# A one-core hybrid pooling / SSD encoder step: gate products in the other pool of PSUM banks, two pool tiles' sums behind gate splits, and a new order for the last piece's scalings and the last tile's weights

## The chip, the cores and the metric

The kernel runs on one core of one Trainium2 chip. The metric is the device time of one execution in microseconds (us). Engine names are those of the profile: PE multiplies matrices (TensorE; PEld is its weight load), DVE is VectorE, ACT is ScalarE, POOL is GpSimd, and SP issues most of the DMAs. PSUM is the memory that PE writes its products to. It is used here as eight banks of 128 x 512 float32, and a product occupies one bank until DVE or ACT has read it.

## The reference, cut to what matters

One layer of a streaming encoder for 384 tokens (256 of a new stream and 8 x 16 of running streams), width 2048, all in float32:

```
u = RMSNorm(x); P = u @ w_in                 # columns: pool | z | xBC | dt | gates
pool branch: for windows 2, 4, 8, 16 (four groups of 512 channels)
  d = windowed mean of p - p; a = (d @ pool_w[g]) * pool_scale
SSD branch: causal conv, Mamba-2 scan, gated RMSNorm
m = sigmoid(g_A) * (a @ w_pool_proj) + sigmoid(g_B) * (a_ssd @ w_ssd_proj)
x += RMSNorm(m @ w_out)
x += RMSNorm(relu(RMSNorm(x) @ w_up)^2 @ w_down)
outputs: y (384 x 2048), new pooling, conv and SSM states
```

## The kernel before

**Products.** Each float32 operand is cut into a high and a low part (`h`, `l`) of a type that PE takes at full rate, and each product is three matmuls: `h*h`, `h*l`, `l*h`. Activations are cut once. Weights are cut as they stream in: `wfetch` has SP fetch 128 x 1024 elements into one of three buffers of the tag `w`; `wsplit` has ACT write the high part (`wh`, line 72) and DVE the low part (`wl`, line 73), three buffers each. A product of 384 columns is 128 channels by 384 tokens (`proj`, two halves of 24 matmuls); its matmuls are lines 100, 101 and 102 of the helper `mm3`.

**Banks.** Two pools share PSUM in the first half: `mmtile` hands out two banks in turn and `sstile` six. `proj` takes its bank from whatever `bank[0]` holds, which is `mmtile` at the start.

**Pool and gate stage.** Five of the sixteen tiles of the pooling input (`early`, p0 to p4) are multiplied while the input arrives, in `sstile` banks. `pool_tile(gi, k4)` takes tile k = 4*gi + k4: DVE scales it out of its bank by the norm (lines 379 to 381), ACT copies states in and out, DVE makes the window sums (396), the difference from the mean (399 to 412) and the split (415 on ACT, 416 on DVE). `pool_map(g)` multiplies group g's four tiles by `pool_w[g]`. `gate_a(i)` multiplies gate tile i (`pj_ga`), scales it out of its bank (439) and takes the sigmoid. The program has tiles 0 to 3, tiles 4 and 5 (p5 is the first product of this stage in an `mmtile` bank), gates 0 to 3, then `pool_map(0)`.

**Order.** Instructions are recorded in the program's order and a list scheduler then sets each engine's order from dependencies and its own costs. `behind(ins)` tells it to issue something only after `ins` on that engine; `later()` does so behind the latest weight split on ACT and on DVE. On each engine the resulting order is fixed, and an instruction that waits holds up all behind it.

**The MLP's second product.** `w_down` is multiplied by a scheme with fewer products than the plain one, in eight chunks of 1024 rows and column pieces; `blocks(c, sb, w)` does one piece. Its splits have letters (a, b, c, d, e, f, g; ACT line 1363, DVE line 1364), its matmuls are lines 1377 to 1379, its banks X, Y, M and `c3`. `evict` adds a bank to `acc` (1386); the sums `t2 = w21 + t2` are line 1330. In the last chunk, `blocks(7, 0)`, a finished 128 x 512 block is also tallied: `tally` has ACT square and sum it (1310) and DVE multiply it by the post-norm's gain `gpo` (1313).

**The last two column blocks** (nb = 2 and 3) are multiplied plainly, with `w_tail`: four weight units each (`wt2_0` to `wt2_3`, `wt3_0` to `wt3_3`; matmul lines 1495 to 1497). For nb = 3 two units go to `wpool`, and units 2 and 3 are fetched there but cut into buffers of their own (`e_wt3_2`, `e_wt3_3`, lines 1519 and 1520). The products of nb = 3 are ordered by token block b = 0, 1, 2; behind each, `tally` finishes block b: `acc` (1305), the square, the gain, the norm and four outputs (1325) with their DMAs (1326).

Of the kernel before, what the change touches and what calls it, by code (L numbers as in the profile page):

```python
# [10 lines left out]
ALU = mybir.AluOpType  # L11
# [22 lines left out]
def build(ctx, tc, io):  # L34
# [93 lines left out]
    def proj(units, rhs, name, hook=None):  # L128
        o = bank[0](f"pj_{name}")[:, :T]
        for q, src in enumerate(units):  # L130
            half(o, q, take(src, f"{name}_{q}"), rhs)
            if hook:
                hook()
        return o
# [223 lines left out]
    with tc.tile_pool(name="phc", bufs=1, reuse_waits="tile") as pc, tc.tile_pool(name="phc2", bufs=2, reuse_waits="tile") as pc2:  # L358
# [9 lines left out]
        ]  # L368
        dd = [[None] * 4 for _ in range(4)]

        def pool_tile(gi, k4):
            w = WINDOWS[gi]
            k = gi * 4 + k4
            ps = early[k] if k < 5 else proj(in_units(1 + k), xg, f"p{k}")
            bf = bufs[k % 2]
            pv = bf[:, 15:271]
            sv = bf[:, 271:].rearrange("p (b t) -> p b t", b=NB)
            po = even_odd(ps)
            v.tensor_tensor(pv[:, :192], po[:, 0], rstd[:, :192], ALU.mult)
            v.tensor_tensor(pv[:, 192:], po[:, 1, :64], rstd[:, 192:TP], ALU.mult)  # L380
            v.tensor_tensor(
                sv[:, :, 15:],
                po[:, 1, 64:].rearrange("p (b t) -> p b t", b=NB),
                rstd[:, TP:].rearrange("p (b t) -> p b t", b=NB),
                ALU.mult,
            )
            s.copy(sv[:, :, :15], pst[:, k])
            stg = pc2.tile([P, 9, 15], F32, tag="stg", name=f"pstg{k}")
            s.copy(stg[:, 0, :], bf[:, 256:271])
            s.copy(stg[:, 1:, :], sv[:, :, 16:])  # L390
            gp.dma_start(io["new_pool"][k], stg)
            cur, sh = bf, 1
            while sh < w:
                nx = pc2.tile([P, 519], F32, tag="win", name=f"win{k}_{sh}")
                lo = 2 * sh - 1
                v.tensor_tensor(nx[:, lo:], cur[:, lo:], cur[:, lo - sh : 519 - sh], ALU.add)
                cur, sh = nx, sh * 2
            d = pc2.tile([P, T], F32, tag="d", name=f"d{k}")
            v.scalar_tensor_tensor(
                out=d[:, :TP], in0=cur[:, 15:271], scalar=1.0 / w, in1=pv, op0=ALU.mult, op1=ALU.subtract  # L400
            )
            v.scalar_tensor_tensor(
                out=d[:, TP:].rearrange("p (b t) -> p b t", b=NB),
                in0=cur[:, 271:].rearrange("p (b t) -> p b t", b=NB)[:, :, 15:],
                scalar=1.0 / w,
                in1=sv[:, :, 15:],
                op0=ALU.mult,
                op1=ALU.subtract,
            )
            rc = cst[:, C_RC + gi * 16 : C_RC + gi * 16 + 16]  # L410
            v.tensor_tensor(d[:, :16], cur[:, 15:31], rc, ALU.mult)
            v.tensor_tensor(d[:, :16], d[:, :16], pv[:, :16], ALU.subtract)
            h = pc.tile([P, T], F32R, tag=f"dh{k4}", name=f"dh{k}", bufs=1)
            l = pc.tile([P, T], F32R, tag=f"dl{k4}", name=f"dl{k}", bufs=1)
            s.activation(h, d, AF.Copy)
            v.tensor_tensor(l, d, h.bitcast(F32), ALU.subtract)
            dd[gi][k4] = (h, l)
# [15 lines left out]
                        out=al, in0=even_odd(o), scalar=sc, in1=ah.bitcast(F32), op0=ALU.mult, op1=ALU.subtract  # L433
                    )

        def gate_a(i):
            ps = proj([io["w_ga"][i, q] for q in range(2)], xg, f"ga{i}")
            sg = pc2.tile([P, T], F32, tag="sg", name=f"sg{i}", bufs=5)
            v.tensor_tensor(halves(sg), even_odd(ps), halves(rstd), ALU.mult)
            s.activation(sg, sg, AF.Sigmoid)  # L440
            return sg
# [76 lines left out]

        for gi in range(4):
            for k4 in range(4):  # L520
                pool_tile(gi, k4)
                if gi and k4 == (gi == 1):
                    if gi == 1:
                        sg = [gate_a(i) for i in range(4)]
                    pool_map(gi - 1, last[0])
        srcs = dt_phase(pc)
        pool_map(3)
# [713 lines left out]
    with ExitStack() as mlp:  # L1241
# [108 lines left out]
        def blocks(c, sb, w):  # L1350
# [16 lines left out]
            def run(hl, ps, *terms):  # L1367
                wh, wl = hl
                with behind(last[0]):
                    for out, j, start in terms:  # L1370
                        for p in ps:
# [6 lines left out]
                            te.matmul(o, h[:, t], vl, start=False, stop=False, skip_group_check=True)  # L1378
                            last[0] = te.matmul(o, l[:, t], vh, start=False, stop=False, skip_group_check=True)  # L1379

            def evict(b, j, src, op=ALU.add, first=False, done=False):
                dst = acc[:, b, blk(2 * sb + j)]
                if first and c == 0:
                    s.activation(dst, src, AF.Copy, scale=-1.0 if op == ALU.subtract else 1.0)
                else:
                    v.tensor_tensor(dst, dst, src, op)
                if done and c == NC - 1:
                    tally(b, 2 * sb + j, dst)

            M = mmtile(f"m{nm}")  # L1390
            a, t, b = (X, H11, True), (Y, S1, True), (M, H12, True)
# [12 lines left out]
            run(t1_, (3,), t)  # L1404
            run(b1, (3,), b, rb)
            if c == NC - 1:
                tally(2, 2 * sb, A)
            d0, d1 = split(t2, 0, "d"), split(t2, 1, "d")
            run(d0, (0, 1), (X, S2, False))
            evict(0, 1, Y, first=True)  # L1410
# [1 line left out]
            run(d1, (2, 3), (X, S2, False))  # L1412
            evict(1, 1, X, ALU.subtract, first=True)
            e0, e1 = split(w["12"], 0, "e"), split(w["12"], 1, "e")
            run(e0, (0, 1), (B, H31, c == 0))
            run(e1, (2, 3), (B, H31, False))
            run(e0, (0, 1), (X, S3, False))
# [6 lines left out]
            f1 = split(w["22"], 1, "f")  # L1424
            run(f1, (2, 3), (B, H3, False), (Y, S4, False))
            if c == NC - 1:
                tally(2, 2 * sb + 1, B)
            evict(1, 1, Y, done=True)
            for u in (0, 1):
                run(split(t2, u, "g"), (2 * u, 2 * u + 1), (X, H22, False))  # L1430
            evict(0, 0, X, first=True, done=True)

        for f in range(3):
            up(f)
# [45 lines left out]
        def lhs(i):  # L1480
# [2 lines left out]
            e = [extra[0][:, i // 2 * 256 + q : i // 2 * 256 + q + P] for q in (0, P)]  # L1483
            return [e if j is None else (h[:, j * P : j * P + P], l[:, j * P : j * P + P]) for j in js]

        for nb in (2, 3):
            o = [mmtile(f"wt{nb}_{b}") if nb == 2 else psd.tile([P, 512], F32, tag="XY"[b], name=f"wt{nb}_{b}") for b in range(2)]
            o.append(c3[nb])
# [12 lines left out]
            if nb == 2:  # L1501
                for kp in range(4):
                    hl = wload(units[kp], names[kp])
                    with behind(last[0]):
                        for i in (2 * kp, 2 * kp + 1):
                            for b in range(3):
                                mm(b, hl, i)
                for b in range(3):
                    tally(b, nb, o[b], b < 2)
                continue  # L1510
            w = []
            for kp in range(4):
                f_, name = wfetch(units[kp], names[kp])
                if kp < 2:
                    w.append(wsplit((f_, name)))
                    continue
                t = pr.tile([P, 2048], F32R, tag=f"t{kp - 1}", name=f"e_{name}")
                h, l = t[:, :1024], t[:, 1024:]
                s.activation(h, f_, AF.Copy)
                v.tensor_tensor(l, f_, h.bitcast(F32), ALU.subtract)  # L1520
                w.append((h, l))
            for b in range(3):
                with behind(last[0]):
                    for i in range(8):
# [125 lines left out]
```

## Time and profile before

| | us |
|---|---|
| median of 3 runs (2621.88 to 2622.18) | 2621.91 |
| the profiled execution's own time | 2624.44 |
| its span, first to last instruction | 2622.7 |
| PE busy | 2606.7 |
| DVE busy | 1775.3 |
| ACT busy | 1302.9 |
| mean granted PE clock (share of full) | 0.998 |

Rows of the timeline read: start, duration, engine, line, operation, output<-inputs, shapes, count, and in brackets the idle time before it with what ended it. PE's matmuls overlap, so a matmul's row is longer than its step to the next start. A row of the waits reads: who waited, for whom, us in total, times, longest.

### The profile page before, as it was taken

To read this page: it belongs to the slowest core of one execution; us is meant where nothing else is said; L and a number is where in the kernel's file an instruction comes from. 1 tells how busy PE (TensorE), PEld (TensorE's weight loads), DVE (VectorE), ACT (ScalarE), POOL (GpSimd) and SP (SyncE) were. 2 spreads that over 40 slices of the span, in tenths; PEclk is the share of its full clock that TensorE was granted. 3 is DMA by queue.
4 is the path that set the end of the run, shared out by engine and by line. 5 is a ranking of instruction groups with operands and counts; after the bars stand their busy time and mean duration, and the time that the engine had idled before them with its cause. 6 is when DMAs were issued, how large, how long until landed. Compare 5 with 4: busy or idle time off the path is not lost.

```text
span 2622.7 us, 40313 instructions
## 1 busy us (share of the span) xinstructions
PE 2606.7 (99%) x15999; PEld 2508.9 (96%) x15999; DVE 1775.3 (68%) x2383; ACT 1302.9 (50%) x1981; POOL 185.8 (7%) x264
## 2 busy tenths in 40 slices
PE   9999999999999999999999999999999999999998
PEld 8999999999999999999999998999999999999997
DVE  6676334778888887876444434766676868677677
ACT  6434225566666575744423334645454545445454
POOL 0000000001111111111000000000000000000000
PEclk9999999999999999999999999999999999999999
DMA  7444445566656666666644455543433444444343
GB/s 276 141 132 159 146 145 199 177 216 208 234 195 226 204 237 204 208 219 228 216 156 160 160 193 169 205 141 129 145 129 131 163 153 141 138 145 144 129 164 118
DMA packets 139420, 457.76 MB, mean 175 GB/s; under 512 B 17568, under 2 KB 44768, under 8 KB 125792
## 3 DMA queue, kind: packets, MB, share of 16 engines
q1 hardware_dynamic: 117120, 326.98, 38.6%
q0 software_dynamic: 22112, 128.21, 13.3%
q8 instruction: 126, 2.06, 0.3%
q14 instruction: 62, 0.51, 0.1%
HBM read 410.26 MB, written 44.86 MB: 174 GB/s over the span
## 4 chain that ended last, share of the span: by engine, by line
PE 96%; DVE 2%; ACT 1%; issue 1%; DMA 1%; POOL 0%; ACTq 0%; POOLq 0%; DVEq 0%
PE pj_up L100 6%; PE pj_up L102 6%; PE pj_up L101 6%; PE pj_x L100 4%; PE pj_x L102 4%; PE pj_x L101 4%; PE pj_z L100 3%; PE pj_z L101 3%; PE pj_sp L102 3%; PE pj_sp L101 3%; PE pj_sp L100 3%; PE pj_z L102 3%; PE c L1378 2%; PE c L1379 2%; PE X L1378 2%; PE X L1379 2%
## 5 line engine op out<-in xcount | busy, mean ns | idle before, releaser
L100 PE MATMUL pj_up<-x1h,wh_up 128*128 128x384 f32 (+1 forms) x1024 | 333.9, 326 | 0.0
L102 PE MATMUL pj_up<-x1h,wl_up 128*128 128x384 f32 (+1 forms) x1024 | 333.7, 326 | 0.0
L101 PE MATMUL pj_up<-x1l,wh_up 128*128 128x384 f32 (+1 forms) x1024 | 333.7, 326 | 0.0
L100 PE MATMUL pj_x<-xgh,wh_x 128*128 128x384 f32 x768 | 252.0, 328 | 0.0
L102 PE MATMUL pj_x<-xgh,wl_x 128*128 128x384 f32 x768 | 250.6, 326 | 0.9 <-DVE wl_x L73 0.9
L101 PE MATMUL pj_x<-xgl,wh_x 128*128 128x384 f32 x768 | 250.4, 326 | 0.0
L72 ACT ACTIVATE wh_up<-w_up 128x1024 fp32r<-128x1024 f32 x126 | 133.1, 1056 | 189.7 <-PE pj_up L101 113.8
L101 PEld LDWEIGHTS pj_up<-x1l,wh_up 128*128 128x128 f32 x1024 | 193.5, 189 | 0.4
L100 PEld LDWEIGHTS pj_up<-x1h,wh_up 128*128 128x128 f32 x1024 | 193.5, 189 | 0.4
L102 PEld LDWEIGHTS pj_up<-x1h,wl_up 128*128 128x128 f32 x1024 | 193.5, 189 | 0.0
L73 DVE TENSOR_TENSOR wl_up<-w_up,wh_up 128x1024 fp32r<-128x1024 f32 x126 | 153.6, 1220 | 58.3 <-ACT wh_up L72 57.3
L101 PE MATMUL pj_z<-xgl,wh_z 128*128 128x384 f32 x512 | 166.9, 326 | 0.0
L100 PE MATMUL pj_sp<-abh,wh_sp 128*128 128x384 f32 x512 | 166.9, 326 | 0.0
L102 PE MATMUL pj_sp<-abh,wl_sp 128*128 128x384 f32 x512 | 166.9, 326 | 0.0
L101 PE MATMUL pj_sp<-abl,wh_sp 128*128 128x384 f32 x512 | 166.9, 326 | 0.0
L102 PE MATMUL pj_z<-xgh,wl_z 128*128 128x384 f32 x512 | 166.9, 326 | 0.0
L100 PE MATMUL pj_z<-xgh,wh_z 128*128 128x384 f32 x512 | 166.9, 326 | 0.0
L73 DVE TENSOR_TENSOR wl_sp<-w_sp,wh_sp 128x1024 fp32r<-128x1024 f32 x64 | 78.2, 1222 | 116.7 <-ACT wh_sp L72 116.7
L72 ACT ACTIVATE wh_x<-w_x 128x1024 fp32r<-128x1024 f32 x96 | 101.0, 1052 | 107.0 <-PE pj_z L101 53.0
L73 DVE TENSOR_TENSOR wl_x<-w_x,wh_x 128x1024 fp32r<-128x1024 f32 x96 | 117.2, 1221 | 51.4 <-ACT wh_x L72 51.4
L72 ACT ACTIVATE wh_sp<-w_sp 128x1024 fp32r<-128x1024 f32 x64 | 67.8, 1059 | 166.4 <-PE pj_sp L101 158.3
L100 PEld LDWEIGHTS pj_x<-xgh,wh_x 128*128 128x128 f32 x768 | 145.1, 189 | 2.6 <-issue 0.4
(455 smaller groups left out, 7114.6 us busy)
## 6 DMA issues: line engine op xcount, KB each, us to landing
w_up<-w_up SPq DMA_DIRECT2D x128, 512.0 KB, 3.5
w<-w_dn POOLq DMA_DIRECT2D x60, 1024.0 KB, 5.2
w_x<-w_in SPq DMA_DIRECT2D x96, 512.0 KB, 3.9
w_z<-w_in SPq DMA_DIRECT2D x64, 512.0 KB, 3.5
w_sp<-w_ssd SPq DMA_DIRECT2D x64, 512.0 KB, 3.5
w_ga<-w_ga SPq DMA_DIRECT2D x32, 512.0 KB, 3.5
w_pp<-w_pp SPq DMA_DIRECT2D x32, 512.0 KB, 3.5
hs<-ssm POOLq DMA_DIRECT2D x16, 1024.0 KB, 6.8
```

The costliest lines, as they stand in the source:

```text
L72: cut[0] = s.activation(h, w, AF.Copy)
L73: cut[1] = v.tensor_tensor(l, w, h.bitcast(F32), ALU.subtract)
L100: te.matmul(out, wh, xh, start=first, stop=False, **how)
L101: te.matmul(out, wh, xl, start=False, stop=False, **how)
L102: return te.matmul(out, wl, xh, start=False, stop=last, **how)
L1378: te.matmul(o, h[:, t], vl, start=False, stop=False, skip_group_check=True)
L1379: last[0] = te.matmul(o, l[:, t], vh, start=False, stop=False, skip_group_check=True)
```

## The change

There are three edits.

1. **Gates in the larger pool, two tiles' sums behind gate splits.** The product of p5 is made first, on its own. Gates 0 to 3 then take `sstile` banks. `gate_a` takes a step that runs after its second half, behind that half's split: tile 4's sums are recorded after the second split of gate 1, tile 5's after that of gate 2.
2. **The last piece's scalings.** `evict` no longer tallies at once; it notes what is due, and `settle` tallies behind the latest low-part split, at three places of `blocks`: after e's splits, after g's second split, and at the end.
3. **The last tile's weights.** Units 2 and 3 of nb = 3 are fetched into `spare`, which takes the space of the piece's `w11`, ahead of the loop, and are cut (`own_units`) behind the split of `wt2_1`. The tallies of nb = 2 stand behind the splits of nb = 3.

```
-        def pool_tile(gi, k4):
+        def pool_proj(k):
+            return early[k] if k < 5 else proj(in_units(1 + k), xg, f"p{k}")
+
+        def pool_tile(gi, k4, ps=None):
...
-            ps = early[k] if k < 5 else proj(in_units(1 + k), xg, f"p{k}")
+            ps = pool_proj(k) if ps is None else ps
...
-        def gate_a(i):
-            ps = proj([io["w_ga"][i, q] for q in range(2)], xg, f"ga{i}")
+        def gate_a(i, step=None):
+            todo = [None, step]
+
+            def hook():
+                step = todo.pop(0)
+                if step:
+                    with later():
+                        step()
+
+            ps = proj([io["w_ga"][i, q] for q in range(2)], xg, f"ga{i}", hook)
...
         for gi in range(4):
             for k4 in range(4):
+                if gi == 1 and k4 < 2:
+                    if k4 == 0:
+                        continue
+                    ps = pool_proj(5)
+                    bank[0] = sstile
+                    steps = [None, lambda: pool_tile(1, 0), lambda: pool_tile(1, 1, ps), None]
+                    sg = [gate_a(i, steps[i]) for i in range(4)]
+                    bank[0] = mmtile
+                    pool_map(0, last[0])
+                    continue
                 pool_tile(gi, k4)
-                if gi and k4 == (gi == 1):
-                    if gi == 1:
-                        sg = [gate_a(i) for i in range(4)]
+                if gi > 1 and k4 == 0:
                     pool_map(gi - 1, last[0])
...
+            due = []
+
+            def settle():
+                with behind(low[0]):
+                    while due:
+                        tally(*due.pop(0))
...
                 if done and c == NC - 1:
-                    tally(b, 2 * sb + j, dst)
+                    due.append((b, 2 * sb + j, dst))
...
             if c == NC - 1:
-                tally(2, 2 * sb, A)
+                due.append((2, 2 * sb, A))
...
             e0, e1 = split(w["12"], 0, "e"), split(w["12"], 1, "e")
+            settle()
...
-                tally(2, 2 * sb + 1, B)
+                due.append((2, 2 * sb + 1, B))
             evict(1, 1, Y, done=True)
             for u in (0, 1):
-                run(split(t2, u, "g"), (2 * u, 2 * u + 1), (X, H22, False))
+                g = split(t2, u, "g")
+                if u:
+                    settle()
+                run(g, (2 * u, 2 * u + 1), (X, H22, False))
             evict(0, 0, X, first=True, done=True)
+            settle()
...
+        own = []
+        spare = pr.tile([P, 2048], F32, tag="w11", name="wt3_f")
+        for kp in (2, 3):
+            sy.dma_start(spare[:, both[kp - 2]], io["w_tail"][1, kp])
+
+        def own_units():
+            for kp in (2, 3):
+                t = pr.tile([P, 2048], F32R, tag=f"t{kp - 1}", name=f"e_wt3_{kp}")
+                h, l = t[:, :1024], t[:, 1024:]
+                cut[0] = s.activation(h, spare[:, both[kp - 2]], AF.Copy)
+                cut[1] = v.tensor_tensor(l, spare[:, both[kp - 2]], h.bitcast(F32), ALU.subtract)
+                own.append((h, l))
...
-                for b in range(3):
-                    tally(b, nb, o[b], b < 2)
+                    if kp == 1:
+                        with later():
+                            own_units()
+                w = [wload(io["w_tail"][1, kp], f"wt3_{kp}") for kp in range(2)] + own
+                with later():
+                    for b in range(3):
+                        tally(b, nb, o[b], b < 2)
                 continue
```

What is computed is the same. How the change moves instructions is shown at three places. The number at a name's end is the program's own; line numbers differ by file.

**DVE in the gate stage**, from the last sums of tile 3 (`d3`) to the low part of gate 2's first half. Before:

```order
L411 TENSOR_TENSOR d3_729<-win3_1_727,cst_69 128x16
L379 TENSOR_TENSOR pbuf0_626<-pj_p4_534,rstd_171 128x192
...
L379 TENSOR_TENSOR pbuf1_628<-pj_p5_759,rstd_171 128x192
...
L381 TENSOR_TENSOR pbuf1_628<-pj_p5_759,rstd_171 128x8x16
...
L439 TENSOR_TENSOR sg0_902<-pj_ga0_841,rstd_171 128x384
L396 TENSOR_TENSOR win5_2_830<-win5_1_828 128x516
L73 TENSOR_TENSOR wl_ga1_1_939<-w_ga1_1_936,wh_ga1_1_938 128x1024
...
L73 TENSOR_TENSOR wl_ga2_0_973<-w_ga2_0_970,wh_ga2_0_972 128x1024
```

The changed kernel:

```order
L414 TENSOR_TENSOR d3_729<-win3_1_727,cst_69 128x16
L73 TENSOR_TENSOR wl_ga1_1_897<-w_ga1_1_894,wh_ga1_1_896 128x1024
...
L382 TENSOR_TENSOR pbuf0_626<-pj_p4_534,rstd_171 128x192
L450 TENSOR_TENSOR sg0_860<-pj_ga0_799,rstd_171 128x384
...
L73 TENSOR_TENSOR wl_ga2_0_952<-w_ga2_0_949,wh_ga2_0_951 128x1024
...
L73 TENSOR_TENSOR wl_ga2_1_982<-w_ga2_1_979,wh_ga2_1_981 128x1024
L382 TENSOR_TENSOR pbuf1_628<-pj_p5_738,rstd_171 128x192
```

The three gate splits now stand ahead of tile 5's reading of its bank (`pbuf1<-pj_p5`), and gate 1's second split ahead of tile 4's.

**DVE and PE in the last piece**, `blocks(7, 0)`, from e's splits to f's (`z2<-c3_0,gpo2` and `acc<-acc,gpo2` are the scalings). DVE before:

```order
L1386 TENSOR_TENSOR acc_16911<-acc_16911,m7_0_24221 128x512
L1313 TENSOR_TENSOR z2_24214<-c3_0_16927,gpo2_24211 128x512
L1364 TENSOR_TENSOR wl_e7_0_0_24337<-w12_7_0_23883,wh_e7_0_0_24336 128x1024
L1313 TENSOR_TENSOR acc_16911<-acc_16911,gpo2_24211 128x512
L1386 TENSOR_TENSOR acc_16911<-acc_16911,X7_0_24219 128x512
L1364 TENSOR_TENSOR wl_e7_0_1_24341<-w12_7_0_23883,wh_e7_0_1_24340 128x1024
L1330 TENSOR_TENSOR t2_7_0_23891<-w21_7_0_23884,t2_7_0_23891 128x1024 x2
L1364 TENSOR_TENSOR wl_f7_0_0_24375<-w22_7_0_23885,wh_f7_0_0_24374 128x1024
```

DVE of the changed kernel:

```order
L1412 TENSOR_TENSOR acc_16911<-acc_16911,m7_0_24221 128x512
L1383 TENSOR_TENSOR wl_e7_0_0_24331<-w12_7_0_23883,wh_e7_0_0_24330 128x1024
L1383 TENSOR_TENSOR wl_e7_0_1_24335<-w12_7_0_23883,wh_e7_0_1_24334 128x1024
L1412 TENSOR_TENSOR acc_16911<-acc_16911,X7_0_24219 128x512
L1332 TENSOR_TENSOR z2_24214<-c3_0_16927,gpo2_24211 128x512
L1332 TENSOR_TENSOR acc_16911<-acc_16911,gpo2_24211 128x512
L1349 TENSOR_TENSOR t2_7_0_23891<-w21_7_0_23884,t2_7_0_23891 128x1024 x2
L1383 TENSOR_TENSOR wl_f7_0_0_24372<-w22_7_0_23885,wh_f7_0_0_24371 128x1024
```

Both splits of e move ahead of the scalings; what stands ahead of f's first split is the same set of instructions as before. PE of the changed kernel, at f's first matmuls:

```order
L1396 MATMUL c3_1_16928<-wh_f7_0_0_24371,hh28_23989 128x512
L1396 MATMUL Y7_0_24220<-wh_f7_0_0_24371,hh28_23989 128x512
L1397 MATMUL c3_1_16928<-wl_f7_0_0_24372,hh28_23989 128x512
L1398 MATMUL c3_1_16928<-wh_f7_0_0_24371,hl28_23990 128x512
L1396 MATMUL c3_1_16928<-wh_f7_0_0_24371,hh29_24100 128x512
```

Before, all six matmuls into `c3_1` came ahead of the first into `Y7_0`; now one of `Y7_0` that needs no low part stands second. This is PE's only difference in order.

**DVE at the last tile's weights**, from the split of `wt2_1` on. Before:

```order
L73 TENSOR_TENSOR wl_wt2_1_24466<-w_wt2_1_24463,wh_wt2_1_24465 128x1024
...
L73 TENSOR_TENSOR wl_wt2_2_24490<-w_wt2_2_24487,wh_wt2_2_24489 128x1024
...
L73 TENSOR_TENSOR wl_wt2_3_24514<-w_wt2_3_24511,wh_wt2_3_24513 128x1024
L73 TENSOR_TENSOR wl_wt3_0_24551<-w_wt3_0_24548,wh_wt3_0_24550 128x1024
L73 TENSOR_TENSOR wl_wt3_1_24557<-w_wt3_1_24554,wh_wt3_1_24556 128x1024
L1520 TENSOR_TENSOR e_wt3_2_24562<-w_wt3_2_24560,e_wt3_2_24562 128x1024
```

The changed kernel:

```order
L73 TENSOR_TENSOR wl_wt2_1_24469<-w_wt2_1_24466,wh_wt2_1_24468 128x1024
L1412 TENSOR_TENSOR acc_16911<-acc_16911,X7_0_24219 128x512
L1527 TENSOR_TENSOR e_wt3_2_24490<-wt3_f_24437,e_wt3_2_24490 128x1024
L1332 TENSOR_TENSOR acc_16911<-acc_16911,gpo2_24211 128x512
L1527 TENSOR_TENSOR e_wt3_3_24493<-wt3_f_24437,e_wt3_3_24493 128x1024
L73 TENSOR_TENSOR wl_wt2_2_24499<-w_wt2_2_24496,wh_wt2_2_24498 128x1024
L73 TENSOR_TENSOR wl_wt2_3_24523<-w_wt2_3_24520,wh_wt2_3_24522 128x1024
```

Both own splits (`e_wt3_2`, `e_wt3_3`) move from behind all others to ahead of `wt2_2`'s; on SP their two loads move from the end of the eight to third and fourth place.

11 lines of the change are left out of this document (removed).

## The prediction

> **What bounds the kernel now.** I read the page's busy times first, then the waits of PE.
>
> ```profile
> PE 2606.7 (99%) x15999; PEld 2508.9 (96%) x15999; DVE 1775.3 (68%) x2383; ACT 1302.9 (50%) x1981; POOL 185.8 (7%) x264
> ```
>
> ```profile
> PE pj_ga L100 <- DVE pbuf L381: 2.6, 1, 2.6
> ...
> PE wt L1496 <- DVE e_wt L1520: 0.8, 1, 0.8
> PE c L1378 <- DVE wl_e L1364: 0.8, 1, 0.8
> ```
>
> PE is busy 99% of the span, so only what makes PE stop, or run slower, can be won. These rows are three of its few waits, one per edit: a gate product waits for the DVE to read p5 out of a bank (edit 1), an own split of the last tile's weights is late (edit 3), a split of piece e is late (edit 2). The rows name only time in which no matmul ran. What a stop really costs I take from PE's starts in the timeline, against the step of an unhindered stretch.
>
> **Edit 1, the gate stage.** PE around the wait:
>
> ```profile
> 62.20 0.33 PE L102 MATMUL pj_ga<-xgh,wl_ga 128*128 128x384 f32 x1
> 65.17 0.66 PE L100 MATMUL pj_ga<-xgh,wh_ga 128*128 128x384 f32 x1 [2.64 <-DVE pbuf L381]
> 65.62 0.53 PE L101 MATMUL pj_ga<-xgl,wh_ga 128*128 128x384 f32 x1
> ...
> 68.18 0.38 PE L100 MATMUL pj_ga<-xgh,wh_ga 128*128 128x384 f32 x1
> 68.39 0.33 PE L101 MATMUL pj_ga<-xgl,wh_ga 128*128 128x384 f32 x1
> ```
>
> ```profile
> 65.20:68.20 3.00, 3.00 (x10) 3.00 (x11) 3.00 (x8) 1.98 (x4) 0.54 (x1) 0.50 0.10 29
> ```
>
> The second row is from the table of windows; its third number from the end is the granted clock, 0.50. From 65.62 to 68.18 eight matmuls take 2.56 us, 0.32 each. The usual step is 7.80 us / 48 = 0.1625. So 11 matmuls took 68.39 - 62.20 = 6.19 us where 11 x 0.1625 = 1.79 would do: **the wait costs 4.40 us**, of which some 1.5 are the half clock behind it.
>
> The Trainium skill (page TensorE: Matmul & The Clock Gate, section Why this matters for your kernels) asks only that PE have no idle gap over about 3 us, one idle window, before the clock falls. This trace disagrees: 2.64 us of idle sufficed. By the page the half clock would not be the wait's, and this term would be some 1.5 us less; that is the third rival below.
>
> Does the wait go? DVE before:
>
> ```profile
> 58.78 0.28 DVE L381 TENSOR_TENSOR pbuf<-pj_p,rstd 128x128 f32<-128x128 f32 x1
> ...
> 64.74 0.28 DVE L381 TENSOR_TENSOR pbuf<-pj_p,rstd 128x128 f32<-128x128 f32 x1
> ...
> 66.72 0.68 DVE L396 TENSOR_TENSOR win<-win 128x516 f32<-128x516 f32 x1
> 67.33 1.22 DVE L73 TENSOR_TENSOR wl_ga<-w_ga,wh_ga 128x1024 fp32r<-128x1024 f32 x1
> ...
> 69.08 1.22 DVE L73 TENSOR_TENSOR wl_ga<-w_ga,wh_ga 128x1024 fp32r<-128x1024 f32 x1
> ```
>
> Gate 1 waited until p5's last read, 64.74 + 0.28 = 65.02. In the larger pool gates 0 to 3 follow tiles p0 to p3, whose last read ends at 58.78 + 0.28 = 59.06; gate 1 wants its bank at 62.20 + 0.16 = 62.36 and gate 3 at 62.36 + 15.6 = 77.96. No bank is late. Next could be a split. Gate 1's second half is wanted at 62.36 + 3.90 = 66.26; its low part, at 67.33 before, now stands directly behind tile 3's last sums and would end by 63.2, cover 3 us. Gate 2's first half is wanted at 70.16; its low part ended at 69.08 + 1.22 = 70.30 with both tiles' sums ahead of it. Four window sums of the step 0.61 (66.72 to 67.33) leave from ahead of it, so it ends at 67.9 at the latest, cover 2.2 us. Tile 4's and 5's reads, sums, ACT copies and output DMAs (POOL, two issues) come a few us later, but their splits cannot go to their buffers until `pool_map(0)` has read the old ones, after gate 3: nothing waits for them earlier. p5 keeps its small bank to about 70 us; the second small bank is free for p6. The sums' removal from the path costs nothing as long as DVE is less than 2.2 us late. **Term: -4.40.**
>
> **Edit 2, the last piece.** PE, then DVE:
>
> ```profile
> 2566.44 0.38 PE L1377 MATMUL c<-wh_e,hh 128*128 128x512 f32 x1
> 2566.97 0.48 PE L1378 MATMUL c<-wl_e,hh 128*128 128x512 f32 x1
> ...
> 2569.84 0.38 PE L1377 MATMUL c<-wh_e,hh 128*128 128x512 f32 x1
> ```
>
> ```profile
> 2565.10 0.68 DVE L1313 TENSOR_TENSOR z<-c,gpo 128x512 f32<-128x512 f32 x1
> 2565.70 1.21 DVE L1364 TENSOR_TENSOR wl_e<-w,wh_e 128x1024 fp32r<-128x1024 f32 x1
> ...
> 2568.03 1.22 DVE L1364 TENSOR_TENSOR wl_e<-w,wh_e 128x1024 fp32r<-128x1024 f32 x1
> 2569.17 2.35 DVE L1330 TENSOR_TENSOR t<-w,t 128x1024 f32<-128x1024 f32 x2
> 2571.44 2.35 DVE L1364 TENSOR_TENSOR wl_f<-w,wh_f 128x1024 fp32r<-128x1024 f32 x2
> ```
>
> Nine matmuls took 3.40 us; at the step of 0.216 they need 1.94: the two late splits cost 1.46. Now e's first split stands one scaling (0.60) earlier, ending 2565.10 + 1.21 = 2566.31, against a want at 2566.44 + 0.22 = 2566.66; the second follows directly, ends by 2567.46 and is wanted at 2567.95. ACT loses one square ahead of its second cut. Both waits go.
>
> But DVE is packed here, and the scalings only move to ahead of f's first split: the same instructions precede it, so it still ends at 2571.44 + 1.22 = 2572.66. PE gets there earlier: 2566.44 + 24 x 0.216 = 2571.62, plus the two matmuls that need no low part, 2572.05. It waits again, to about 2572.72 (PE started 0.06 behind the first e split), and the first step behind a wait is 0.1 longer: 0.77 back. **Term: -1.46 + 0.77 = -0.69.** Bounds: -1.46 if f's split came in time, 0 if the wait moved whole. Behind it there is cover, by DVE's steps of 1.14 for a split (2568.03 to 2569.17) and 0.60 for a scaling or an eviction. f's second split comes 1.74 behind the first, while ten matmuls (2.2 us) stand before its want. The thinnest cover is at the first unit of nb = 2: behind f's first split (2572.6) stand three splits and four short ones, 5.8 us, then `wt2_0`'s, which ends near 2579.7. PE enters nb = 2 at 2580.8 before (89 matmuls of 0.216 ahead of the 2600.05 below), now 0.7 earlier, and wants that low part at 2580.4: cover 0.7 us, and what is missing of it is paid.
>
> **Edit 3, the last tile's weights.**
>
> ```profile
> 2600.05 0.38 PE L1497 MATMUL wt<-e_wt,hl 128*128 128x512 f32 x1
> 2600.74 0.48 PE L1495 MATMUL wt<-e_wt,h 128*128 128x512 f32 x1 [0.30 <-ACT e_wt L1519]
> 2602.05 0.48 PE L1496 MATMUL wt<-e_wt,h 128*128 128x512 f32 x1 [0.83 <-DVE e_wt L1520]
> 2602.37 0.38 PE L1497 MATMUL wt<-e_wt,h 128*128 128x512 f32 x1
> ```
>
> Three matmuls took 2.32 us instead of 0.65: 1.67 lost. Both own splits now follow `wt2_1`'s: by the same steps, two scalings or evictions and that split behind `wt2_0`'s 2579.6 bring DVE to 2581.9, and the two end by 2584.9, where PE wants them after 2598. They stand in front of `wt2_2`'s split, which ends near 2586.1; PE wants it near 2588 (36 matmuls of 0.216 behind 2580.2). Cover 2 us; each us beyond is paid in full. **Term: -1.67.** Is it paid out at the end?
>
> ```profile
> 2603.43 0.69 DVE L1305 TENSOR_TENSOR acc<-acc,wt 128x512 f32<-128x512 f32 x1 [1.44 <-PE wt L1497]
> ...
> 2609.34 0.68 DVE L1305 TENSOR_TENSOR acc<-acc,wt 128x512 f32<-128x512 f32 x1
> ```
>
> The end is a DVE chain that starts with token block 0's product at 2603.43, and block 1's tally follows without idle: 5.9 us per block, where PE needs 24 x 0.216 = 5.2. The chain starts when PE finishes block 0, and all three stops lie before that. It moves by the whole sum.
>
> **Sum:** -4.40 - 0.69 - 1.67 = -6.76 us. The profiled execution took 2624.44 us (span 2622.7 and 1.7 around it) and would take 2617.7; its profile makes it 2.5 slower than the median of the runs. On the median: 2621.91 - 6.76 = **2615.2 us**.
>
> **Rivals.**
> - *f's split is in time too* (the scheduler's extra matmul, or DVE steps a little shorter): the whole 1.46 stays, 2614.4. Against it: DVE's rows run back to back. 10%.
> - *The gate stage still stops PE*, at a split or a bank now held by another reader: edit 1 gives nothing, 2619.6. For it: DVE carries both tiles' sums there and was the late engine; against it: covers of 2 to 3 us. 10%.
> - *The half clock isn't the wait's* and is met elsewhere: 2616.6. For it, the page's rule; against it, the 0.50 sits directly behind the gap. 8%.
> - *The last tile's weights still stop PE*, the own splits and scalings in front making `wt2_0` or `wt2_2` late by as much as edit 3 gains: 2615.2 + 1.67 = 2616.8. For it, the cover of 0.7; against it, it takes 2.4 us more of DVE than the steps say. 7%.
> - *Slower.* On SP the two early loads stand ahead of `wt2_2`'s and wait for POOL's loads into `x1r`:
>
> ```profile
> L1477 POOL DMA_DIRECT2D x1r<-x_scr x3: 527/527/537, 2549.4 to 2550.5; - x3
> ...
> DMA to landing us min/median/max: 6.6/9.3/11.2
> ```
>
>  These end by 2550.5 + 11.2 = 2561.7, so the early loads should land by about 2568. Landing later than 2583, they would hold `wt2_2`'s split on both engines, and each us more is a us of PE. All three gains are eaten from about 2590 on: slower than 2621.9. 5%.
>
> **Numbers.** My forecast has 60%, with its own range 2614.8 to 2616.0. A range of 2614.0 to 2617.2 takes in the first, third and fourth rivals and leaves out the second and the last. A change of 0.2% is 5.2 us, about what a measurement of this kernel can tell. Faster by more: 60% + 10% + half of the third rival, which sits on the bound, 74%. Within: the rest of it, 10% and 7%, 21%. Slower 5%.
>
> **What would show it.** No wait of PE on `pbuf`, and no window with a clock of 0.50 in the gate stage; the waits on `wl_e` replaced by one of about 0.7 on `wl_f`; none on `e_wt`; the time from the first `acc<-acc,wt` of block 0 to the end unchanged at 19.3. I am wrong if a gate half waits for its low part, if f's wait is over 1.2 or gone, or if `wt2_2` stops PE.

## The result

The changed kernel takes 2617.14 us (median of 17 runs, 2616.07 to 2617.82), the kernel before 2622.87 us (17 runs, 2621.29 to 2624.9). The ratio is 0.9977, with a 95% interval from 0.9970 to 0.9985: faster, by 5.73 us. The prediction was 2615.2 us (2614.0 to 2617.2). The time lies at the upper end of the range, 0.06 us inside it, and outside the likeliest case's own one (2614.8 to 2616.0).

The profiled spans moved further than the times: 2622.7 us before, 2615.9 us now. That is the 6.76 us of the sum, to the tenth. How a span can move by 6.8 and a median by 5.7 is the main finding below.

The changed kernel's busy times, and all waits of PE:

```profile
PE 2604.1 (100%) x15999; PEld 2507.5 (96%) x15999; DVE 1775.4 (68%) x2383; ACT 1302.4 (50%) x1981; POOL 185.7 (7%) x264
```

```profile
PE warm_o L234 <- DVE warm L230: 1.2, 1, 1.2
PE pj_x L102 <- DVE wl_x L73: 0.9, 1, 0.9
PE c L1397 <- DVE wl_f L1383: 0.5, 1, 0.5
PE pj_p L310 <- ACT xgh L270: 0.2, 1, 0.2
```

The waits on `pbuf`, `wl_e` and `e_wt` are gone; one on `wl_f` is new. The others belong to the start (`warm`, `xgh`) and to the convolution's products (`wl_x`), which the change does not touch.

**Gate stage.** The two stretches of the table of windows (the granted clock is the third number from the end), then DVE's splits and p5's last reading in the timeline:

```profile
62.50:65.20 2.70, 2.70 (x19) 2.70 (x18) 2.70 (x7) 2.67 (x4) 0.00 (x0) 1.00 0.69 191
65.20:68.20 3.00, 3.00 (x21) 3.00 (x19) 2.90 (x9) 2.22 (x6) 0.54 (x1) 1.00 0.79 228
```

```profile
61.89 1.22 DVE L73 TENSOR_TENSOR wl_ga<-w_ga,wh_ga 128x1024 fp32r<-128x1024 f32 x1
...
64.17 1.22 DVE L73 TENSOR_TENSOR wl_ga<-w_ga,wh_ga 128x1024 fp32r<-128x1024 f32 x1
...
69.63 0.28 DVE L384 TENSOR_TENSOR pbuf<-pj_p,rstd 128x128 f32<-128x128 f32 x1
```

PE is busy without a break and the clock stays at 1.00. Gate 1's second half has its low part at 61.89 + 1.22 = 63.11 (forecast 63.2, wanted at 66.26). Gate 2's first half has it at 65.39, 2.5 us before the latest time that the prediction gave. The last reading of p5 now ends at 69.91, after 65.02 before, and nobody waits for it.

**Last piece.** PE at f's first matmuls, then DVE:

```profile
2567.19 0.38 PE L1396 MATMUL c<-wh_f,hh 128*128 128x512 f32 x1
2567.41 0.38 PE L1396 MATMUL Y<-wh_f,hh 128*128 128x512 f32 x1
2568.28 0.48 PE L1397 MATMUL c<-wl_f,hh 128*128 128x512 f32 x1 [0.49 <-DVE wl_f L1383]
2568.60 0.38 PE L1398 MATMUL c<-wh_f,hl 128*128 128x512 f32 x1
```

```profile
2560.66 2.36 DVE L1383 TENSOR_TENSOR wl_e<-w,wh_e 128x1024 fp32r<-128x1024 f32 x2
...
2567.01 1.22 DVE L1383 TENSOR_TENSOR wl_f<-w,wh_f 128x1024 fp32r<-128x1024 f32 x1
...
2574.05 1.22 DVE L73 TENSOR_TENSOR wl_wt<-w_wt,wh_wt 128x1024 fp32r<-128x1024 f32 x1
...
2580.39 1.22 DVE L73 TENSOR_TENSOR wl_wt<-w_wt,wh_wt 128x1024 fp32r<-128x1024 f32 x1
```

f's first split ends at 2568.23 and PE starts 0.05 later. Three steps take 2568.60 - 2567.19 = 1.41 us where 3 x 0.216 = 0.65 would do: 0.76 given back, forecast 0.77. The third and fourth DVE rows are the low parts of `wt2_0` and `wt2_2`, which end at 2575.27 and 2581.61.

**Last column blocks.** PE's first use of those two low parts is at 2575.94 and 2583.71, so the covers are 0.67 and 2.10 us (forecast 0.7 and 2). The tail on DVE:

```profile
2575.94 0.38 PE L1540 MATMUL wt<-wl_wt,h 128*128 128x512 f32 x1
...
2583.71 0.38 PE L1540 MATMUL wt<-wl_wt,h 128*128 128x512 f32 x1
```

```profile
2596.64 0.69 DVE L1324 TENSOR_TENSOR acc<-acc,wt 128x512 f32<-128x512 f32 x1 [2.46 <-PE wt L1541]
...
2602.55 0.68 DVE L1324 TENSOR_TENSOR acc<-acc,wt 128x512 f32<-128x512 f32 x1
```

From 2596.64 to the end at 2615.9 it is 19.3 us, and 5.91 from block to block, both as before.

### The profile page after: what moved, and what is told of

It is laid out like the page before. It is cut to its first block, busy times and chain, and to the rows that moved or that the text cites. A ratio compares the mean times of both kernels' runs of the same rounds, so it can differ in the third digit from the quotient of the medians.

```text
span 2615.9 us, 40308 instructions
## 1 busy us (share of the span) xinstructions
PE 2604.1 (100%) x15999; PEld 2507.5 (96%) x15999; DVE 1775.4 (68%) x2383; ACT 1302.4 (50%) x1981; POOL 185.7 (7%) x264
## 4 chain that ended last, share of the span: by engine, by line
PE 97%; DVE 1%; ACT 1%; issue 0%; DMA 0%; POOL 0%; ACTq 0%; POOLq 0%
PE pj_up L100 6%; PE pj_up L101 6%; PE pj_up L102 6%; PE pj_x L100 4%; PE pj_x L102 4%; PE pj_x L101 4%; PE pj_z L100 3%; PE pj_sp L102 3%; PE pj_sp L100 3%; PE pj_z L102 3%; PE pj_z L101 3%; PE pj_sp L101 3%; PE c L1397 2%; PE c L1398 2%; PE c L1396 2%; PE X L1397 2%
```

## The experiments

To compare kernels I use PE's **lost time** in a stretch of the program: the sum over its matmuls of the step to the next start, minus the unhindered step (0.1625 us at 384 columns, 0.2158 at 512). One profiled execution of each:

| kernel | span | first 20 us | gates, 60 to 80 us | convolution, 430 to 460 us | from 2540 us on |
|---|---|---|---|---|---|
| before | 2622.7 | 4.91 | 4.40 | 1.54 | 3.13 |
| before, again | 2621.0 | 4.48 | 2.88 | 1.77 | 3.22 |
| changed | 2615.9 | 4.90 | 0.00 | 1.51 | 0.77 |
| changed, again | 2615.5 | 4.07 | 0.00 | 1.95 | 0.77 |
| edit 1 alone | 2617.3 | 4.15 | 0.00 | 1.35 | 3.16 |
| edit 2 alone | 2623.5 | 4.80 | 4.37 | 1.83 | 3.79 |
| edit 2 alone, again | 2620.3 | 3.68 | 2.87 | 1.38 | 3.65 |
| edit 3 alone | 2621.4 | 4.94 | 4.43 | 1.88 | 1.46 |
| larger pool alone | 2619.9 | 4.21 | 1.78 | 1.87 | 3.32 |
| gap filled | 2621.4 | 4.62 | 2.95 | 1.96 | 3.20 |
| changed, first settle behind f | 2615.1 | 4.12 | 0.00 | 2.15 | 0.16 |
| edit 2, last settle behind `wt2_2` | 2621.6 | 4.43 | 2.88 | 2.01 | 3.55 |
| edit 2, two settles behind `wt2_0` | 2621.5 | 4.05 | 4.56 | 1.77 | 2.44 |

(The gap-filled kernel's 2.95 is the time of its 17 added matmuls, 62.07 to 65.03, which are counted as lost.) The first and third columns differ by up to 1.3 and 0.8 us between executions, for stretches that no kernel here changes. That is noise of the single execution; the second and fourth columns carry the edits. That the changed kernel's span fell by just the forecast sum is thus partly chance: its first and third columns happened to equal the first profile's.

### The three edits, one at a time

Edit 1 alone:

```
+                    ps = pool_proj(5)
+                    bank[0] = sstile
+                    steps = [None, lambda: pool_tile(1, 0), lambda: pool_tile(1, 1, ps), None]
+                    sg = [gate_a(i, steps[i]) for i in range(4)]
+                    bank[0] = mmtile
```

> Edit 1 alone (gates in the larger pool, sums of tiles 4 and 5 behind gate splits); edits 2 and 3 undone. My theory: the stop of PE in the gate stage is worth 4.40 us, of which about 1.5 is the half clock behind it, and the terms add up: span 2622.7 - 4.4 = 2618.3, no window with a clock of 0.50 in the gate stage, the stops at wl_e (1.46) and e_wt (1.67) as before. Rival, the half clock is not the wait's: span near 2619.8 and a clock of 0.50 somewhere else after 60 us. Rival, the gains overlap (all three edits only free DVE and the end is set elsewhere): less than 4 or more than 5.

Measured: 2619.81 us against 2622.6 (ratio 0.9988, 0.9979 to 0.9996). From its profile, the waits of PE, without those of the start and of the convolution:

```profile
...
PE wt L1515 <- DVE e_wt L1539: 0.8, 1, 0.8
PE c L1397 <- DVE wl_e L1383: 0.8, 1, 0.8
PE wt L1514 <- ACT e_wt L1538: 0.3, 1, 0.3
...
```

No wait in the gate stage, and the three rows of the other edits are there. The gate column goes from 4.40 to 0.00, the last one stays (3.16). The time gains 2.8; its interval, 1.0 to 5.5, does not tell that from 4.4, and why it is less is shown below.

Edit 2 alone:

```
+            def settle():
+                with behind(low[0]):
+                    while due:
+                        tally(*due.pop(0))
...
             e0, e1 = split(w["12"], 0, "e"), split(w["12"], 1, "e")
+            settle()
...
+                if u:
+                    settle()
...
             evict(0, 0, X, first=True, done=True)
+            settle()
```

> Edit 2 alone (the last piece's scalings settled behind the splits); edits 1 and 3 undone. My theory: the wait on wl_e (1.46) goes and one of 0.75 on wl_f takes its place, DVE being packed: span 2622.7 - 0.7 = 2622.0. Rival, the whole wait is won: 2621.2. Rival, it only moves: 2622.7. The gate stage still stops; whether its half-clock stretch is again about 3 us long or differs shows how far that part varies between executions, and the span is to be read with it.

Measured: 2623.55 us against 2622.6 (1.0003, 0.9994 to 1.0012), and no gain in the profile. From the waits of PE:

```profile
...
PE wt L1507 <- ACT e_wt L1531: 1.7, 1, 1.7
...
PE wt L1508 <- DVE e_wt L1532: 0.8, 1, 0.8
PE c L1378 <- DVE wl_f L1364: 0.5, 1, 0.5
```

At e and f it does what it did in the changed kernel. But the wait for ACT's own split is 1.7 us instead of 0.3, so what was won in the last piece is lost at the last tile, and 0.66 more (3.79 after 3.13). Why is settled below.

Edit 3 alone:

```
+        spare = pr.tile([P, 2048], F32, tag="w11", name="wt3_f")
+        for kp in (2, 3):
+            sy.dma_start(spare[:, both[kp - 2]], io["w_tail"][1, kp])
...
+                    if kp == 1:
+                        with later():
+                            own_units()
```

> Edit 3 alone (units 2 and 3 of the last tile fetched into their own space and cut early); edits 1 and 2 undone. My theory: the two stops on e_wt (1.67) go and nothing replaces them, and the DVE chain at the end starts 1.67 earlier with its 19.3 unchanged: span 2622.7 - 1.7 = 2621.0. Rival, the two splits and the scalings make wt2_0 or wt2_2 late: a wait of PE there and less than 1 us won. The gate stage's half-clock stretch is to be read beside it as in the kernel with edit 2 alone.

Measured: 2621.62 us against 2622.6 (0.9996, 0.9988 to 1.0005). From the waits of PE, and the stretch behind the gap:

```profile
PE pj_ga L100 <- DVE pbuf L381: 2.6, 1, 2.6
...
PE c L1378 <- DVE wl_e L1364: 0.8, 1, 0.8
```

```profile
65.20:68.20 3.00, 3.00 (x9) 3.00 (x10) 3.00 (x8) 1.99 (x4) 0.54 (x1) 0.50 0.10 29
```

No wait on `e_wt`. The last column goes from 3.13 to 1.46, which is the 1.67 of the forecast; what is left is piece e's two stops.

### The gate stage: bank, order and clock

The gates in the larger pool, with both tiles' sums where they were:

```
+                        bank[0] = sstile
                         sg = [gate_a(i) for i in range(4)]
+                        bank[0] = mmtile
```

> Half of edit 1: gates 0 to 3 take their banks from the larger pool, but tiles 4 and 5 are summed in the old place, ahead of the gate splits, so DVE's order is that of the kernel before. My theory: the bank is no longer late, but gate 1's second half is (its low part still ends at 67.33 + 1.22 = 68.55 where PE, with two matmuls of gate 2 pulled ahead, wants it at 66.9): a stop of 1.6 to 1.7 us on wl_ga in place of 2.6. If the half clock comes only from the longer gap, the net gain is 4.4 - 1.8 = 2.6, span 2620.1; if 1.6 us of idle is enough for it, about 1.5 less, span 2621.6. Rival, the bank was the whole of it: span 2618.3 and no wait.

Measured: 2621.52 us against 2622.6 (0.9994, 0.9986 to 1.0003). PE and the second stretch:

```profile
67.89 0.43 PE L102 MATMUL pj_ga<-xgh,wl_ga 128*128 128x384 f32 x1 [1.53 <-DVE wl_ga L73]
```

```profile
65.20:68.20 3.00, 1.47 (x10) 1.18 (x9) 3.00 (x7) 2.53 (x4) 0.28 (x1) 1.00 0.07 23
```

The bank's wait is gone and a split's has come: gate 1's second low part stands behind the sums, as the 67.33 of the kernel before had shown. It costs 1.78. So the pool of banks gives 4.40 - 1.78 = 2.62 of the first profile's term, and the order of the sums the rest. (Against the 2.88 that the same stop costs without a half clock, as shown below, it gives 1.10.) A gap of 1.53 us leaves the clock at 1.00.

The kernel before, with 17 matmuls that nobody reads put into the gap:

```
+                        fill = sstile("fill")[:, :T]
+                        with behind(last[0]):
+                            for _ in range(17):
+                                last[0] = te.matmul(fill, xg[0][0][:, :P], xg[0][1], start=True, stop=True)
...
```

> The kernel before with the wait left in place but filled: 17 matmuls of 384 columns, into a spare bank that nobody reads, run on PE between gate 0 and gate 1 (17 x 0.1625 = 2.76 us of the 2.81 us gap). Work is added, none is left out. My theory: the half clock is set off by the idle gap, so it goes, and the gap itself stays: span 2622.7 - 1.5 = 2621.2, clock 1.00 in the stretch behind the gap. Rival, the half clock has another cause (load, a free-running throttle): clock 0.50 there or nearby as before, span 2622.7.

Measured: 2623.08 us against 2622.49 (1.0001, 0.9992 to 1.0010); the profile has:

```profile
65.20:68.20 3.00, 3.00 (x20) 3.00 (x20) 3.00 (x8) 2.10 (x3) 0.54 (x1) 1.00 0.07 23
```

With PE busy through the gap there is no half clock behind it. The time did not fall by the 1.5 us that this seemed to be worth, however. The next runs show why such a gain can be expected in a part of the executions only; what is then left of it, these times cannot tell.

Both kernels once more, without any edit, on the same chip:

> The kernel before itself, for a second profile. My theory: the gap in the gate stage is 2.6 us again, but the half-clock stretch behind it varies between executions (the runs of the kernel before spread over 3.6 us, those of the changed kernel over 1.8): a stretch between 0 and 3.4 us long, span between 2621.2 and 2622.9. Rival, it is always 3.0 us and the spread has another cause: span 2622.7 within 0.1.

> The changed kernel itself, for a second profile and for times on the same chip as the kernel with the settling behind f. Expected: span 2615.9, ratio to the kernel before 0.9974 to 0.998.

Measured: the kernel before 2623.55 us and the changed one 2616.95 us, against 2622.49 (1.0003, 0.9994 to 1.0012; 0.9977, 0.9968 to 0.9986). The kernel before, in its second profile:

```profile
64.74 0.40 PE L100 MATMUL pj_ga<-xgh,wh_ga 128*128 128x384 f32 x1 [2.65 <-DVE pbuf L381]
64.98 0.33 PE L101 MATMUL pj_ga<-xgl,wh_ga 128*128 128x384 f32 x1
```

```profile
65.20:68.20 3.00, 3.00 (x20) 3.00 (x19) 3.00 (x7) 2.10 (x3) 0.54 (x1) 1.00 0.09 29
```

The same gap, 2.65 us, and **no half clock**: 20 matmuls in the stretch instead of 10, and the stop costs 2.88 instead of 4.40. Of the seven profiles with this gap, four show the half clock behind it (cost 4.37 to 4.56) and three do not (2.87 or 2.88).

The traces also show what decides. The granted clock changes on a grid. Between two changes, the stretches at full clock in the 13 profiles are 54.61, 58.03, 2546.34, 2549.76, 2600.96, 2604.37, 2607.78 or 2611.20 us long, which is 16, 17, 746, 747 and 762 to 765 times 3.4133 us. Each half clock in the gate stage lasts one such step. Against the program, the grid lies elsewhere in each execution. Two steps of the first profile, then one of the second (length, then PE's busy time; the clock is again the third number from the end):

```profile
61.45:64.86 3.41, 1.08 (x7) 0.78 (x5) 3.41 (x13) 2.17 (x6) 0.54 (x1) 1.00 0.50 184
64.86:68.28 3.42, 3.11 (x10) 3.14 (x11) 3.42 (x9) 2.21 (x4) 0.54 (x1) 0.50 0.09 25
```

```profile
60.59:64.01 3.42, 1.50 (x10) 1.20 (x8) 3.42 (x13) 2.29 (x7) 0.54 (x1) 1.00 0.61 174
```

In the first profile PE is idle for 2.34 us of one step, and the next step is at half clock. In the second a border of the grid cuts the gap into 1.92 and 0.73 us, and the clock stays. In the four profiles with the half clock, 2.25 to 2.65 us of the gap lie within one step; in the three others 1.92 at most. The end of the program, where PE has no work left, fits in all 13: the clock falls behind the first step with 2.07 us of idle time or more, and not behind one with 1.88 or less. So the limit lies between 1.92 and 2.07 us of idle time in one step, and a gap of 1.53 us cannot reach it.

The mean granted clock, which is known for most executions, finds only some of these. A mean below 0.999 occurred in 55 of 167 executions of the kernels that have the 2.65 us gap, and in none of 71 executions of the kernels that have a shorter one or none. But the last kernel of the table has the half clock in its profile at a mean of 0.999. The end of every profiled execution runs at half clock too, 3.6 us there and 4.7 in the first profile, and this decides the third digit. So at least one execution in three of the kernel before pays for the half clock. If the grid falls evenly, it is 56 to 65% of them: an estimate from the two limits, (3.41 + 2.65 - 2 x 2.07) / 3.41 and the same with 1.92. The changed kernel has no such gap, and neither of its two profiles shows a half clock in the gate stage.

In the four groups of runs of the kernel before, the executions with a mean below 0.999 have medians of 2624.05 to 2624.62 us and the others of 2622.26 to 2622.53, a difference of 1.8 to 2.3 us. The profiles put 1.5 to 1.7 of it down to the half clock itself. The three profiles with a mean of 0.998 also lost more in the first 20 us (4.80 to 4.94) than the four others with this gap (3.69 to 4.48); why is not shown.

### Why edit 2 alone gives nothing

My first theory was a square: in edit 2 alone, ACT has one of them, waiting 2.60 us for `acc<-acc,X`, ahead of the cut of `wt2_2`. One run moves that last settle behind the splits of `wt2_2` (shown against edit 2 alone):

```
             evict(0, 0, X, first=True, done=True)
-            settle()
+            return settle
...
                     hl = wload(units[kp], names[kp])
+                    if kp == 2:
+                        with later():
+                            settle()
```

> Edit 2 alone, but the last settle (the square and the scaling of the block that X finishes) is called behind the splits of wt2_2 instead of at the end of the piece, so that ACT cuts wt2_2 ahead of that square, as in the kernel before. Theory: with edit 2 alone it was this square, waiting 2.60 us for acc<-acc,X in front of the cut of wt2_2 (2583.55 against 2582.00 before), that made all later loads into the three w buffers late and the own split e_wt3_3 0.79 us later than before (2600.43 against 2599.64). Then the cut comes at 2582.0 or earlier, e_wt3_3 at 2599.64 or earlier, the ACT wait on e_wt is at most 1.0 instead of 1.66, and the loss from 2540 us on is 3.13 (if the loads keep their times) down to 2.44 (if they move with PE) instead of 3.79. Rival: the scalings on DVE around wt2_0 and wt2_1 make the loads late: then the ACT wait stays near 1.7 and the loss at 3.8. The time follows by at most 1.4 us, about what 11 executions can tell.

> Edit 2 alone once more, beside the run above on the same chip. Theory: the square stands in front of the cut of wt2_2 again, ACT wait on e_wt about 1.7 us, loss from 2540 us on 3.8, time 0.7 to 1.4 us above the run above. In the gate stage the gap of 2.65 us is followed by a granted clock of 0.5 in some executions and not in others: a mean clock of 0.998 in about 3 of 10 executions, and these 1.5 to 2 us longer. Rival: the loss differs from one execution to the next and falls to 3.1.

Measured: 2623.54 and 2622.74 us against 2623.6 (1.0002, 0.9993 to 1.0011; 0.9999, 0.9990 to 1.0008). The wait for ACT's own split in the two, first the moved square, then edit 2 again:

```profile
PE wt L1507 <- ACT e_wt L1534: 1.4, 1, 1.4
```

```profile
PE wt L1507 <- ACT e_wt L1531: 1.5, 1, 1.5
```

A difference of 0.1, with 3.55 and 3.65 lost at the end: the square is not the cause. It stands ahead of the cut, but the cut would wait for its load anyway. What makes the load late is in DVE's and SP's rows. The kernel before, the low part of `wt2_0`, then the loads of `wt2_2` (the first of the merged pair) and `wt3_2`:

```profile
2577.18 1.21 DVE L73 TENSOR_TENSOR wl_wt<-w_wt,wh_wt 128x1024 fp32r<-128x1024 f32 x1
...
2578.42 2.75 SPq L65 DMA_DIRECT2D w_wt<-w_tail  x2
...
2591.21 0.33 SPq L65 DMA_DIRECT2D w_wt<-w_tail  x1
```

Edit 2 alone, the same three, and then ACT's cuts of the two own units:

```profile
2578.61 1.22 DVE L73 TENSOR_TENSOR wl_wt<-w_wt,wh_wt 128x1024 fp32r<-128x1024 f32 x1
...
2579.90 0.33 SPq L65 DMA_DIRECT2D w_wt<-w_tail  x1
...
2591.83 0.33 SPq L65 DMA_DIRECT2D w_wt<-w_tail  x1
...
2595.39 1.06 ACT L1531 ACTIVATE e_wt<-w_wt 128x1024 fp32r<-128x1024 f32 x1 [2.20 <-DMA w_wt<-w_tail]
...
2600.43 1.04 ACT L1531 ACTIVATE e_wt<-w_wt 128x1024 fp32r<-128x1024 f32 x1
```

Each of these loads leaves 0.02 to 0.07 us behind the low part of the unit two places earlier (2577.18 + 1.21 = 2578.39, load at 2578.42; 2578.61 + 1.22 = 2579.83, load at 2579.90). Edit 2 moves a scaling (`z<-c,gpo`) and an eviction (`acc<-acc,Y`) ahead of `wt2_0`'s low part. That comes 1.44 later, so `wt2_2`'s load leaves 1.48 later. The chain of loads and cuts makes up part of that; `wt3_2`'s load is still 0.62 late. Its cut, the evictions and squares of nb = 2 and the other own cut stand in line behind it, so the second one starts at 2600.43 instead of 2599.64. So the next run takes these out of `wt2_0`'s way (shown against edit 2 alone):

```
                 g = split(t2, u, "g")
-                if u:
-                    settle()
...
             evict(0, 0, X, first=True, done=True)
-            settle()
+            return settle
...
                     hl = wload(units[kp], names[kp])
+                    if kp == 0:
+                        with later():
+                            settle()
```

> Edit 2 alone, but only its first settle stays in the piece; what the second and the last would do (three scalings, three squares) is called behind the splits of wt2_0, so that DVE makes wt2_0's low part directly behind g's second split. Each of the last six loads of w_tail leaves 0.02 to 0.07 us behind the low split of the unit two places earlier. Theory: with edit 2 alone wt2_0's low part ended at 2579.83 instead of 2578.39 before, so wt2_2's load left at 2579.90 instead of 2578.42, and wt3_2's at 2591.83 instead of 2591.21; e_wt3_2, the evictions and squares of nb = 2 and e_wt3_3 stand behind that load, and the tail's clock is the loads' and not PE's. Then wt2_0's low part ends at least 1.3 us earlier than in edit 2 alone, the ACT wait on e_wt is 0.3 to 1.0 instead of 1.5 to 1.7, and the loss from 2540 us on is 2.44 to 3.1 instead of 3.65 to 3.79. Rival: the loads are not what holds the own splits; then the wait stays at 1.4 or more and the loss at 3.5 or more. Time: at most 1.2 us below edit 2 alone.

Measured: 2623.27 us against 2623.18 (0.9998, 0.9989 to 1.0007). The times cannot tell 0.7 us here; the profile can. The low part of `wt2_0`, the load behind it, and three of PE's waits:

```profile
2576.09 1.22 DVE L73 TENSOR_TENSOR wl_wt<-w_wt,wh_wt 128x1024 fp32r<-128x1024 f32 x1
...
2577.33 3.96 SPq L65 DMA_DIRECT2D w_wt<-w_tail  x2
```

```profile
...
PE wt L1506 <- DVE e_wt L1533: 0.8, 1, 0.8
PE c L1378 <- DVE wl_f L1364: 0.5, 1, 0.5
PE wt L1505 <- ACT e_wt L1532: 0.3, 1, 0.3
```

The low part ends at 2577.31 and the load leaves at 2577.33. The wait for ACT is back at 0.3, and the loss at the end is 2.44 = 3.13 - 0.69, the whole of the forecast's term. So the late loads were the cause, and DVE's order made them late. In the changed kernel edit 3 hides it: the two own units no longer come through these buffers.

### The wait on f

The changed kernel with its first settle behind f's splits instead of e's:

```
             e0, e1 = split(w["12"], 0, "e"), split(w["12"], 1, "e")
-            settle()
...
             f1 = split(w["22"], 1, "f")
+            settle()
```

> The changed kernel with the first settling of the scalings moved from behind e's splits to behind f's splits. My theory: DVE is packed between e and g and only the order decides which split is late; with the scalings behind f's splits, f's first low part ends 1.2 us earlier, PE's wait on wl_f (0.75) goes, g's splits still come in time by about 0.9 and wt2_0's by nearly nothing: span 2615.9 - 0.75 = 2615.2, with at most 0.2 of wait on wt2_0. Rival, DVE is the bound there whatever the order: the wait moves on to wl_g or wt2_0 with most of its 0.75 and the span stays 2615.9.

Measured: 2616.82 us against 2622.49 (0.9977, 0.9968 to 0.9986), beside the changed kernel's 2616.95. All of PE's waits:

```profile
PE pj_x L102 <- DVE wl_x L73: 1.4, 2, 0.9
PE warm_o L234 <- DVE warm L230: 1.2, 1, 1.2
PE pj_p L102 <- DVE wl_e L296: 0.7, 1, 0.7
PE pj_p L310 <- ACT xgh L270: 0.3, 1, 0.3
PE pj_p L310 <- DVE xgl L272: 0.2, 1, 0.2
```

None is left in the last piece or behind it, and the loss at the end falls from 0.77 to 0.16. So f's stop was the two scalings' and nothing else's. This is the best kernel by its profile, by 0.61 us; the times do not tell it from the changed one.

## Why the prediction was right, and where it was not

- **Edit 1, that the wait goes:** right. No bank and no split is late, and the covers were as large as said or larger. The run with the bank alone shows that both halves of the edit are needed.
- **Edit 1, the size -4.40:** this is the step that failed. The term was read from one execution that had the half clock, and it is 2.88 in an execution without. The prediction took it from a base that most likely had none: the three executions behind 2621.91 took 2622.18 us or less, and no execution of this kernel with a mean clock known to be below 0.999 took less than 2622.67. The 2.5 us by which the profiled execution was slower the prediction put down to the profile. It was not the profile: the second profiled execution of the kernel before took 2622.76 us, below its own group's median of 2623.55. The first one was one of the dearer executions. Its sum is -6.76; with 2.88 the sum is -5.24. Over all executions on record the kernel before has a mean of 2623.07 us (129) and the changed one of 2617.05 (27). The difference of 6.02 lies between the two sums, as it must if a part of the executions has the half clock; a share of 56 to 65% would make 5.24 + 0.56 to 0.65 x 1.52, 6.1 to 6.2.
- **The third rival** (the half clock is not the wait's) is refuted: in the gate stage it came in no profile without the gap, and where it came it followed the step with the gap. But its sum, with a term 1.5 smaller, was nearer the time, because the clock does not follow every gap.
- **The base:** the other part of the miss. Three runs of the kernel before gave 2621.91, seventeen gave 2622.87; 0.96 of the 1.9 us between forecast and time is that. The rest, 1.0, is the sum's: 6.76 forecast, 5.73 measured.
- **The range:** that it holds the time is partly luck. Its upper bound, 2617.2, was set to take in the first, third and fourth rivals; none of them happened, and the two errors above ended 0.06 us below it.
- **Edit 2:** right in the changed kernel (e's stops gone, 0.76 back at f for 0.77, `wt2_0`'s cover 0.67 for 0.7). The prediction priced that cover only for PE's want of the low part; that the same split also lets the load of `wt2_2` go was not seen. Alone, the edit loses all of its gain by that.
- **Edit 3:** right, 1.67 alone and in the whole, and the 19.3 us tail moves as one piece.
- **The other rivals:** f's split in time, gates still stopped, and last weights still stopped did not happen. SP's two early loads left within a microsecond of 2548.85 and held nothing up.

## What to carry to other kernels

A stop's price from one profile holds for that execution: look at the granted clock behind the gap in more than one profile before the price is carried to a median. The mean clock of an execution shows the dearer kind only in part. When a split moves back in its engine's order, ask not only who reads its result but whose buffer it frees: a load may leave only when that split ends. And two edits can be worth more together than apart, so an edit that gives nothing alone may still belong in the change.

## What was not expected of the hardware

- A gap of 2.64 to 2.65 us on PE is followed by one step of 3.41 us at a granted clock of 0.50 in some executions of the same program and by 1.00 in others (four and three profiles). What decides is how much of the gap falls into one step of the grid on which the clock changes: 2.25 us or more in the four, 1.92 or less in the three. A gap of 1.53 us left the clock at 1.00 in its one profile, and none of that kernel's 11 executions has a mean below 0.999. The Trainium skill (page TensorE: Matmul & The Clock Gate, section Part 1: The HAM clock gate (the "warmup" mystery)) says that the clock falls after at least one idle window of about 3.4 us and that the window is free-running. The runs disagree with the length, since 2.07 us of idle time in a step were enough. They agree with the free-running window: the steps are 3.413 us long and lie elsewhere against the program in each execution.
- The first step behind a stop is longer even at full clock: 64.98 - 64.74 = 0.24 us instead of 0.1625 at 384 columns, 0.32 instead of 0.216 at 512 (2568.28 to 2568.60).
- The stretches that no kernel here changes differ by up to 1.3 us (first 20 us) and 0.8 us (convolution) between executions. A gain of 0.7 us can be read in a profile's rows at its place, while eleven times of a kernel do not show it.
